# Two delays of a hand-written planner in a one-core decoder layer: the first attention scores come one block later, the first group-norm transposes ask for a later slot

## The chip, the cores and the metric

The kernel runs on one core of a Trainium2 chip. The metric is device time in microseconds, from the start of the execution to its end on that core. Three runs of the kernel before took 410.61, 412.03 and 411.76 us; their median is 411.76 us. One more execution was profiled, and all rows below are from it.

## The reference

One decoder layer is computed for 256 tokens of width 1024. Two kinds of token mixing run side by side on one normalised input: a recurrence with 8 heads (RWKV-7) and softmax attention with 8 heads; a merge with gates, an output projection and a gated MLP follow. The parts that the change touches, shortened:

```python
def step(state, inp):                      # one token of the recurrence
    r_t, w_t, k_t, v_t, a_t, b_t = inp
    sa = jnp.einsum('bhvk,bhk->bhv', state, a_t)
    state = (state * w_t[:, :, None, :] + sa[..., None] * b_t[:, :, None, :]
             + v_t[..., None] * k_t[:, :, None, :])
    return state, jnp.einsum('bhvk,bhk->bhv', state, r_t)
...
mu = jnp.mean(y, axis=-1, keepdims=True)   # group norm over each head's 64 values
var = jnp.mean(jnp.square(y - mu), axis=-1, keepdims=True)
y = ((y - mu) * lax.rsqrt(var + GN_EPS)).reshape(B, S, C)
y = y * ln_g.astype(f32) + ln_b.astype(f32)
...
s_own = jnp.einsum('bhqd,bhkd->bhqk', q_c, k_own, preferred_element_type=f32) * scale
s_own = jnp.where(causal, s_own, -jnp.inf)
p = jax.nn.softmax(s_all, axis=-1).astype(v.dtype)
```

With 256 tokens there is one attention block, so the attention is plain causal attention over 256 keys.

## The kernel before

**The streamed products.** Every large product is made from weights that stream from HBM in pieces of 512 KB (tile raw). ScalarE rounds a piece to a high part (tile whi, L259), VectorE takes the rest as a low part (tile wlo, L269), and TensorE multiplies both. In the stretch that matters here the products go through wst (L293): one call of its inner loop is a **block** of 12 matmuls, eight of L302 and L304 on the high part and four of L307 on the low part, 128x256 each. A piece of weights gives two blocks. The blocks in this stretch are the gate projections (tile acc, input hx), afterwards the attention's branch projection (input ybh). Buffers are few: 4 of raw, 4 of whi, 3 of wlo.

**The side work.** Between the blocks TensorE gets small matmuls, with VectorE and ScalarE working on their results:

- chain (L551), the recurrence in chunks of 64 tokens. It first inverts small triangular matrices (tile X). L765 multiplies X by G into pp, L770 masks pp into P on VectorE, L782 and L790 multiply P and X into px, and L775 adds px to X on VectorE. Then come four steps, c = 0 to 3. In each, L890 and L895 multiply the state Sn, L898 adds the result to Z0 on VectorE, L902 multiplies Z0 by X, L905 (ScalarE) and L906 (VectorE) copy that to VU, L912 and L924 multiply VU, L917 to L920 make the next state Sn on VectorE, and L929 (ScalarE) copies the chunk's output yt. Step 0 has no state yet and begins at L902.
- group_norm (L845), per chunk: sums and means on VectorE (L852, L853, L855), a square on ScalarE (L856), its sum (L858, L859), a power on GpSimd (L860), the scaling on VectorE (L862), then two transposes on TensorE into pc (L869) and the finish (L872 to L875), which gives yah and yal, the input of the last branch projection.
- attention (L967): queries and keys are transposed into qkT (L976, copied by ScalarE, L977), four transposes in four places. Scores then come in three parts, the first over the first 128 tokens and 8 heads, the other two over the second 128 tokens and 4 heads each. A part is its matmuls (L995, tile ps), the masking on VectorE (L998) and, for the later parts, a copy on ScalarE (L1001), the row maximum on VectorE (L1006, L1007), one exponential per head on ScalarE (L1010), and the normalisation on VectorE (L1012, L1013). L1023 then transposes the weights into ppt, L1024 copies them on ScalarE, and L1035 applies them into po.

**What sets the order.** Three Python generators (chain, gn for the group norm, att for the attention) and bulk, the streamed products, run as threads of a planner at the end of body (L1114 and after). Each yield gives an estimated TensorE cost and a delay. The planner's clock moves by the cost, and the thread may go on once the delay is over. The planner takes the first thread in the list whose time has come, in the order chain, gn, att, bulk; a block of bulk costs 0.33 * 4 = 1.32 units:

```python
cost, lat = next(th[1])
now_t += cost
th[2] = now_t + lat
if cost:
    joined[0] = th[0] != "bulk"
```

So a delay decides after how many blocks a piece of side work is issued, and beside which other side work. The flag joined is true while the last cost came from side work. The group norm holds its transposes until it is true, so that they follow other side work without a block between (L865). TensorE runs its instructions in the planner's order; the order of the instructions on VectorE and ScalarE comes from the same program through the framework's scheduler, and each of these engines runs its own queue in order.

Of the kernel before, what the change touches and what calls it, by code (L numbers as in the profile page):

```python
# [37 lines left out]
def body(tc, x, positions, norm1_g, w_in, rwkv_mu, w_decay_up, decay_bias, w_aaa_up,  # L38
# [5 lines left out]
    with ctx:  # L44
# [12 lines left out]
        def b4(name, shape=(128, 4, 256), dt=F32):  # L57
            return sb.tile(list(shape), dt, name=name, tag="b4", bufs=NB4)
# [5 lines left out]
        def t1(name, shape=(128, 256), dt=F32):  # L64
            return sb.tile(list(shape), dt, name=name, tag="c1", bufs=8)
# [7 lines left out]
        def chp(name="ch"):  # L73
            return ps.tile([128, 512], F32, name=name, tag="ch", bufs=3)

        def atp(name="at"):
            return ps.tile([128, 512], F32, name=name, tag="at", bufs=2)
# [469 lines left out]
        def need(nm, d):  # L547
            while nm not in d:
                yield 0, 0.5

        def chain():  # L551
# [36 lines left out]
            for t in range(2):  # L588
                for ct in range(4):
                    i = 8 * t + 2 * ct  # L590
# [254 lines left out]
            def group_norm():  # L845

                for c in range(4):
                    yield from need(c, ny)
                    y = ny[c]
                    cs = slice(64 * c, 64 * c + 64)  # L850
                    st = sb.tile([128, 3, 4], F32, name="st", tag="st", bufs=2)
                    dve.tensor_reduce(st[:, 0], y, axis=AX.X, op=OP.add)  # L852
                    dve.tensor_scalar(st[:, 0], st[:, 0], -1.0 / N, None, op0=OP.mult)  # L853
                    yc, sq2 = t1("yc", (128, 4, 64)), t1("sq2", (128, 4, 64))
                    dve.tensor_tensor(yc, y, st[:, 0][:, :, None].to_broadcast([128, 4, 64]), op=OP.add)  # L855
                    act.activation(sq2, yc, AF.Square)  # L856
                    yield 0, 0.8
                    dve.tensor_reduce(st[:, 1], sq2, axis=AX.X, op=OP.add)  # L858
                    dve.tensor_scalar(st[:, 1], st[:, 1], N * GN_EPS, None, op0=OP.add)  # L859
                    pool.tensor_tensor(st[:, 2], st[:, 1], mhalf, op=OP.pow)  # L860
                    yield 0, 1.6
                    dve.scalar_tensor_tensor(yc, yc, math.sqrt(N), st[:, 2][:, :, None].to_broadcast([128, 4, 64]),  # L862
                                             op0=OP.mult, op1=OP.mult)
                    yield 0, 1.2 if c < 3 else 2.2
                    while not joined[0] and "chain" not in done:  # L865
                        yield 0, 0.1
                    p = chp("pc").rearrange("p (a n) -> p a n", a=8)
                    for j in range(2):
                        pe.transpose(p[:, 2 * j:2 * j + 2].rearrange("p a n -> p (a n)"),  # L869
                                     yc[:, 2 * j:2 * j + 2].rearrange("p q n -> p (q n)"), ident)  # L870
                    yf = t1("yf", (128, 4, 64))
                    dve.tensor_tensor(yf, p[:, 0:4], A1[:, :, cs], op=OP.mult)  # L872
                    dve.tensor_tensor(yf, yf, A2[:, :, cs], op=OP.add)
                    act.copy(yah_[:, :, cs], yf)
                    dve.tensor_tensor(yal[:, :, cs], yf, yah_[:, :, cs].bitcast(F32), op=OP.subtract)  # L875
                    yield 0.5, 2.0

            threads.insert(1, ["gn", group_norm(), 0.0])
            joined[0] = True
            St = None  # L880
# [83 lines left out]
        def flat3(t):  # L964
            return t.rearrange("p h n -> p (h n)")

        def attention():  # L967
            qkT = []
            for i in range(2):
                dT = b4(f"qkT{i}")  # L970
                for j in range(2):
                    p = atp("pqk").rearrange("p (a t c) -> p a t c", a=2, t=2)
                    for a in range(2):
                        for t in range(2):
                            ct = 2 * j + a
                            pe.transpose(p[:, a, t], flat3(qkv[i][:, t])[:, ct * 128:ct * 128 + 128], ident)  # L976
                    act.copy(dT[:, 2 * j:2 * j + 2].rearrange("p a c -> p (a c)"),  # L977
                             p.rearrange("p a t c -> p (a t c)"))
                    yield 0.4, 1.0
                qkT.append(dT)  # L980
            qT, kT = qkT

# [104 lines left out]
        def bulk():  # L1087
            yield from proj4("k", 4)
            yield from proj4("r", 0)
            def attention_input(i):  # L1090
                qkv.append(b4("qkv", (128, 2, 8, 64)))
                ps_ = [acc(), acc()]
                yield from xst(ps_, hh, hl)
                for t in range(2):
                    finish_qk(ps_[t], i, t)

            while not last_exp:
                yield 0, 0.5
            rope_tables()
            yield from attention_input(0)  # L1100
            yield from proj4("v", 8)
            yield from attention_input(1)
            yield from gates(1, 0)
            yield from attention_input(2)
            threads.insert(1, ["att", attention(), now_t + 3.0])
            for j in range(1, 4):
                yield from gates(1, j)
            for j in range(4):
                yield from gates(0, j)
            while "att" not in done:  # L1110
                yield 0, 1.0
            yield from branch(1, *ybs)
# [155 lines left out]
        j, hb = prev.pop(0)  # L1268
# [47 lines left out]
```

## Time and profile before

| | |
|---|---|
| median of three runs | 411.76 us |
| the profiled execution, its own time | 410.49 us |
| its span in the trace | 408.4 us |
| VectorE busy | 324.8 us (80%) |
| ScalarE busy | 233.0 us (57%) |
| GpSimd busy | 38.8 us (10%) |
| granted TensorE clock | 1.00 in every slice |

The time around the span is 410.49 - 408.4 = 2.1 us. Times in the rows are counted from the span's start. The change touches the stretch from 116 us to 187 us. In a timeline row the first number is the start, the second how long it lasted, then engine, line, operation, output and input tile, the shape, and how many instructions were merged. On TensorE a row's length contains the tail of a matmul in the pipeline, so the step from one piece of work to the next is read from the starts. A float32 matmul of the program shows as two records: 32 matmuls of L782 are x64 in the trace.

### The profile page before, as it was taken

The page shows a single profiled execution, that of the slowest core. Times are in us where ns is not written, and L with a number is a line of the kernel's source. Part 1 is how long each engine was busy: PE and PEld are TensorE (multiplying, and loading weights), DVE is VectorE, ACT ScalarE, POOL GpSimd, SP SyncE. Part 2 cuts the span into 40 slices and gives each one's busy share as a digit, 9 for nine tenths or more (in the row PEclk, how much of TensorE's full clock was granted, in tenths as well). Part 3 has the DMA queues.
Part 4 walks back from the last instruction along what each step waited for, and adds up shares of the span by engine and source line. Part 5 has one row for each costly group of instructions (what it writes and reads, how often), then busy time and mean ns, then how long its engine had stood idle before and what let it go on. Part 6 is the DMA issues. An engine that isn't in the chain of part 4 may idle for free.

```text
span 408.4 us, 8156 instructions
## 1 busy us (share of the span) xinstructions
PE 401.3 (98%) x3199; PEld 354.3 (87%) x3199; DVE 324.8 (80%) x564; ACT 233.0 (57%) x387; POOL 38.8 (10%) x65
## 2 busy tenths in 40 slices
PE   7999999999999999999999999999999999999996
PEld 3999989888989989999988888888888888888885
DVE  3888999899679786777973899968769678697694
ACT  6799655474556756444553876645545555465450
POOL 7910070000400010020010100000000000000000
PEclk9999999999999999999999999999999999999999
DMA  8944555563683353465663556666755666656512
GB/s 246 323 150 154 158 158 160 152 173 99 160 232 92 104 152 104 132 206 189 196 201 115 172 190 202 210 208 184 213 180 167 213 185 201 197 171 207 196 55 103
DMA packets 61990, 70.53 MB, mean 173 GB/s; under 512 B 9421, under 2 KB 52243, under 8 KB 61952
## 3 DMA queue, kind: packets, MB, share of 16 engines
q1 hardware_dynamic: 61104, 69.54, 56.5%
q0 software_dynamic: 832, 0.47, 0.6%
q8 instruction: 25, 0.41, 0.4%
q14 instruction: 13, 0.11, 0.1%
q10 hardware_dynamic: 16, 0.00, 0.0%
HBM read 68.56 MB, written 1.44 MB: 171 GB/s over the span
## 4 chain that ended last, share of the span: by engine, by line
PE 90%; DVE 3%; ACT 3%; issue 2%; DMA 1%; SPq 0%; POOL 0%; DVEq 0%; ACTq 0%
PE acc L1202 15%; PE acc L302 8%; PE acc L1207 8%; PE acc L307 7%; PE acc L304 7%; PE at L1202 5%; PE acc L323 5%; PE acc L327 4%; PE acc L324 4%; PE f L1224 4%; PE f L1222 4%; PE f L1226 4%; PE at L1207 2%; DMA x<-in_x_dram 1%; PE pgr L669 1%
## 5 line engine op out<-in xcount | busy, mean ns | idle before, releaser
L259 ACT CAST whi<-raw 128x1024 fp32r<-128x1024 f32 x121 | 126.9, 1052 | 114.0 <-PE acc L304 22.3
L269 DVE TENSOR_TENSOR wlo<-raw,whi 128x1024 fp32r<-128x1024 f32 x121 | 148.5, 1231 | 30.2 <-PE acc L1207 12.2
L1202 PE MATMUL acc<-hx,whi 128*128 128x512 f32 x264 | 68.2, 393 | 0.0
L302 PE MATMUL acc<-hx,whi 128*128 128x256 f32 x232 | 58.5, 288 | 0.0
L304 PE MATMUL acc<-hx,whi 128*128 128x256 f32 x232 | 56.1, 278 | 0.0
L1202 PEld LDWEIGHTS acc<-hx,whi 128*128 128x128 f32 x264 | 47.0, 188 | 8.1
L302 PEld LDWEIGHTS acc<-hx,whi 128*128 128x128 f32 x232 | 43.6, 188 | 1.8 <-issue 0.8
L304 PEld LDWEIGHTS acc<-hx,whi 128*128 128x128 f32 x232 | 43.7, 188 | 0.1
L1207 PEld LDWEIGHTS acc<-h,wlo 128*128 128x128 f32 x264 | 37.1, 188 | 3.6
L1207 PE MATMUL acc<-h,wlo 128*128 128x256 f32 x264 | 37.9, 279 | 0.0
L307 PE MATMUL acc<-hx,wlo 128*128 128x256 f32 x232 | 35.9, 277 | 0.0
L1224 PE MATMUL f<-whi,hb 128*128 128x512 f32 x80 | 31.2, 390 | 0.0
L1226 PE MATMUL f<-wlo,hb 128*128 128x512 f32 x80 | 31.2, 390 | 0.0
L1222 PE MATMUL f<-whi,hb 128*128 128x512 f32 x80 | 31.2, 389 | 0.0
L307 PEld LDWEIGHTS acc<-hx,wlo 128*128 128x128 f32 x232 | 30.7, 188 | 0.3 <-issue 0.3
L1202 PE MATMUL at<-hx,whi 128*128 128x512 f32 x88 | 24.0, 392 | 0.0
L1212 DVE TENSOR_REDUCE an<-acc 128x256 f32<-128x512 f32 x22 | 14.2, 685 | 9.3 <-PE acc L1207 9.3
L1202 PEld LDWEIGHTS at<-hx,whi 128*128 128x128 f32 x88 | 16.4, 188 | 3.6
L323 PE MATMUL acc<-whi,hx 128*128 128x512 f32 x48 | 19.1, 398 | 0.0
L324 PE MATMUL acc<-whi,hx 128*128 128x512 f32 x48 | 18.8, 391 | 0.0
L1226 PEld LDWEIGHTS f<-wlo,hb 128*128 128x128 f32 x80 | 15.0, 188 | 3.1
L1222 PEld LDWEIGHTS f<-whi,hb 128*128 128x128 f32 x80 | 15.0, 188 | 2.8
(322 smaller groups left out, 695.7 us busy)
## 6 DMA issues: line engine op xcount, KB each, us to landing
raw<-in_w_ffn_up_dram SPq DMA_DIRECT2D x44, 512.0 KB, 4.3
raw<-in_w_in_dram SPq DMA_DIRECT2D x37, 512.0 KB, 4.4
raw<-in_w_ffn_down_dram SPq DMA_DIRECT2D x22, 512.0 KB, 4.1
raw<-in_w_out_dram SPq DMA_DIRECT2D x8, 512.0 KB, 4.3
x<-in_x_dram SPq DMA_DIRECT2D x8, 256.0 KB, 4.0
early<-in_w_in_dram SPq DMA_DIRECT2D x4, 512.0 KB, 7.5
raw<-in_w_branch_b_dram SPq DMA_DIRECT2D x4, 512.0 KB, 3.7
raw<-in_w_branch_a_dram SPq DMA_DIRECT2D x4, 512.0 KB, 4.6
```

The source lines that it names most:

```text
L259: act.copy(wide(hi, k, c), spread(raw, k, c))
L269: eng.tensor_tensor(wide(lo, k, c), spread(raw, k, c), wide(hi, k, c).bitcast(F32), op=OP.subtract)
L302: pe.matmul(om, wh[:, k, ms], xh[:, k0 + k], start=k0 + k + m == 0, stop=False, skip_group_check=True)
L304: pe.matmul(om, wh[:, k, ms], xl[:, k0 + k], start=False, stop=False, skip_group_check=True)
L307: pe.matmul(om, wl[:, k, ms], xh[:, k0 + k], start=False, stop=k0 + k == nk - 1 and m == n - 1, skip_group_check=True)
L323: pe.matmul(ps_[t], xh[:, K, ts], wh[:, k], start=K == 0, stop=False)
L324: pe.matmul(ps_[t], xl[:, K, ts], wh[:, k], start=False, stop=False)
L1202: pe.matmul(ps_[m], wh[:, k, m * 128:m * 128 + 128], hx[:, k0 + k].rearrange("p a s -> p (a s)"), start=k0 + k == 0, stop=False, skip_grou ...
L1207: pe.matmul(ps_[m][:, 0:S], wl[:, k, m * 128:m * 128 + 128], h2[k0 // 4][:, k], start=False, stop=k0 + k == 7, skip_group_check=True)
L1222: pe.matmul(fin[f], hb[:, 0, i, ts], wh[:, 0, cs], start=st, stop=False, skip_group_check=f == 3)
L1224: pe.matmul(fin[f], hb[:, 1, i, ts], wh[:, 0, cs], start=False, stop=False, skip_group_check=f == 3)
L1226: pe.matmul(fin[f], hb[:, 0, i, ts], wl[:, 0, cs], start=False, stop=False, skip_group_check=f == 3)
```

## The change

Two delays of the planner change. No instruction is added, removed or resized. The fourth and last of the attention's query and key transposes (i and j both 1) is followed by a delay of 5.5 in place of 1.0, and the group norm of chunk 0 asks for its transposes 4.0 after its scaling in place of 1.2; chunks 1 to 3 keep theirs.

```diff
@@ -861,7 +861,7 @@
                     yield 0, 1.6
                     dve.scalar_tensor_tensor(yc, yc, math.sqrt(N), st[:, 2][:, :, None].to_broadcast([128, 4, 64]),
                                              op0=OP.mult, op1=OP.mult)
-                    yield 0, 1.2 if c < 3 else 2.2
+                    yield 0, (4.0, 1.2, 1.2, 2.2)[c]
                     while not joined[0] and "chain" not in done:
                         yield 0, 0.1
                     p = chp("pc").rearrange("p (a n) -> p a n", a=8)
@@ -976,7 +976,7 @@
                             pe.transpose(p[:, a, t], flat3(qkv[i][:, t])[:, ct * 128:ct * 128 + 128], ident)
                     act.copy(dT[:, 2 * j:2 * j + 2].rearrange("p a c -> p (a c)"),
                              p.rearrange("p a t c -> p (a t c)"))
-                    yield 0.4, 1.0
+                    yield 0.4, 5.5 if i and j else 1.0
                 qkT.append(dT)
             qT, kT = qkT
```

What moves is seen in the engines' queues. With [B] for a block, TensorE's order from the last L976 on was: [B], scores 1 with L782 and L790, [B] [B], L765 with L790 and scores 2, [B] [B], L790, [B], scores 3, [B], L902, [B] [B], L912 and L924, [B] [B], L890 and L895, [B], L1023 with L902 and L869. It becomes: [B] [B], L782 and L790, [B], scores 1, [B], L765 and L790, [B], scores 2, [B], L790, [B] [B], L902 with scores 3, [B] [B], L912 and L924, [B] [B], L890 and L895, [B] [B], L902 with L1023 and L869. From there on the groups are the same in both, with one block more ahead of them.

The first place is TensorE at the first scores, about 117.7 us. Before, they stood at the head of the recurrence's group:

```order
L307 MATMUL acc<-hx,wlo 128x256 x4
L995 MATMUL ps<-qkT_1572,qkT_1505 128x128 x8
L782 MATMUL px<-P,X 64x64 x32
L790 MATMUL px<-X,P 64x64 x16
L302 MATMUL acc<-hx,whi 128x256
```

After the change the same eight matmuls have a block in front and a block behind; L782 and L790 stand one block ahead of these rows:

```order
L304 MATMUL acc<-hx,whi 128x256
L307 MATMUL acc<-hx,wlo 128x256 x4
L995 MATMUL ps<-qkT_1572,qkT_1505 128x128 x8
L302 MATMUL acc<-hx,whi 128x256
L304 MATMUL acc<-hx,whi 128x256
```

The group of L782 and L790 has gone behind a second block and the first scores another block further, into a place of their own.

The second place is VectorE ahead of L898, the addition to Z0 that L902 of step 1 reads. Before, from the mean's subtraction in the group norm of chunk 0 (L855) on:

```order
L855 TENSOR_TENSOR yc<-yt,st 128x256
L1013 TENSOR_TENSOR sc_1645<-sc_1645,sm 128x1024
L858 TENSOR_REDUCE st<-sq_2015 128x4
L269 TENSOR_TENSOR wlo<-raw,whi 128x1024
L859 TENSOR_SCALAR st<-st 128x4
L898 TENSOR_TENSOR Z_1241<-pb,Z_1241 128x128 x2
L862 SCALAR_TENSOR_TENSOR yc<-yc,st 128x256
```

And after the change (sc_1729 is the scores' tile of parts 2 and 3 there):

```order
L855 TENSOR_TENSOR yc<-yt,st 128x256
L858 TENSOR_REDUCE st<-sq_2027 128x4
L859 TENSOR_SCALAR st<-st 128x4
L862 SCALAR_TENSOR_TENSOR yc<-yc,st 128x256
L1012 RECIPROCAL sm<-sm 128x4
L269 TENSOR_TENSOR wlo<-raw,whi 128x1024
L1013 TENSOR_TENSOR sc_1729<-sc_1729,sm 128x1024
L898 TENSOR_TENSOR Z_1241<-pb,Z_1241 128x128 x2
```

L898 has moved from ahead of the group norm's scaling (L862) to behind it, and behind a low part and the normalisation of the last scores as well.

The third place is TensorE at step 1's L902 and the first transposes of the group norm (L869, tile pc). Before:

```order
L307 MATMUL acc<-hx,wlo 128x256 x4
L1023 MATMUL ppt<-ident,sc 128x128 x8
L902 MATMUL pb<-Z_1241,X 64x64 x8
L869 MATMUL pc<-ident,yc 128x128 x2
L302 MATMUL acc<-hx,whi 128x256
```

And after:

```order
L307 MATMUL acc<-hx,wlo 128x256 x4
L902 MATMUL pb<-Z_1241,X 64x64 x8
L1023 MATMUL ppt<-ident,sc 128x128 x8
L869 MATMUL pc<-ident,yc 128x128 x2
L302 MATMUL acc<-hx,whi 128x256
```

L902 now stands ahead of the transposes of the attention weights, and these stand between L902 and L869. The edit in group_norm alone accounts only for the order of L1023 and L869: with the edit in attention alone the group reads L902, L869, L1023.

## The prediction

> **What bounds the kernel now.** I read the page's busy shares and its chain first, then TensorE's timeline from 116 to 187 us, then those of VectorE and ScalarE.
>
> ```profile
> span 408.4 us, 8156 instructions
> PE 401.3 (98%) x3199; PEld 354.3 (87%) x3199; DVE 324.8 (80%) x564; ACT 233.0 (57%) x387; POOL 38.8 (10%) x65
> PE 90%; DVE 3%; ACT 3%; issue 2%; DMA 1%; SPq 0%; POOL 0%; DVEq 0%; ACTq 0%
> ```
>
> TensorE is busy for 98% of the span and is 90% of the chain that ended last. No work is added, so the change is priced by TensorE's steps and by the waits that it gains or loses. Two waits stand in the stretch that moves:
>
> ```profile
> 117.75 1.16 PE L995 MATMUL ps<-qkT,qkT 64*128 64x128 f32 x16
> 118.84 1.16 PE L782 MATMUL px<-P,X 64*64 64x64 f32 x64
> 119.82 0.86 PE L790 MATMUL px<-X,P 64*64 64x64 f32 x23
> 121.33 0.45 PE L790 MATMUL px<-X,P 64*64 64x64 f32 x9 [0.66 <-issue]
> q8 instruction: 1, 0.02, 1.1%
> 147.34 0.46 PE L902 MATMUL pb<-Z,X 64*64 64x64 f32 x16
> 148.29 0.41 PE L869 MATMUL pc<-ident,yc 128*128 128x128 f32 x2 [0.49 <-DVE yc L862]
> ```
>
> The first, 0.66 us inside L790, has no releaser ("issue"). The q8 row is of the DMA queues between 117 and 123 us: one packet of instructions arrived there. I read the gap as TensorE out of instructions. The second, 0.49 us ahead of L869, waits for the group norm's scaling.
>
> **The steps of TensorE.** These starts give the length of each piece; L302 rows are the first matmul of a block.
>
> ```profile
> 124.66 1.16 PE L765 MATMUL pp<-X,G 64*64 64x64 f32 x64
> 127.73 0.39 PE L302 MATMUL acc<-hx,whi 128*128 128x256 f32 x1
> 130.66 2.08 PE L790 MATMUL px<-X,P 64*64 64x64 f32 x64
> 132.68 0.38 PE L302 MATMUL acc<-hx,whi 128*128 128x256 f32 x1
> 134.25 1.14 PE L995 MATMUL ps<-qkT,qkT 64*128 64x256 f32 x8
> 135.31 0.39 PE L302 MATMUL acc<-hx,whi 128*128 128x256 f32 x1
> 140.24 0.69 PE L912 MATMUL pS<-VU,KBt 128*64 128x64 f32 x16
> 144.88 0.38 PE L302 MATMUL acc<-hx,whi 128*128 128x256 f32 x1
> ```
>
> A lone block between two side groups takes 134.25 - 132.68 = 1.57 us, a pair 130.66 - 127.73 = 2.93. Two lone blocks are 3.14, so splitting a pair costs 0.21. Scores alone take 135.31 - 134.25 = 1.06; L765, L790 and scores together 127.73 - 124.66 = 3.07, so L765 and L790 alone 2.01; a pair and the 64 records of L790 132.68 - 127.73 = 4.95; L912, L924, a pair, L890 and L895 144.88 - 140.24 = 4.64.
>
> **The change part by part.** *One more group.* Before, 17 side groups stand between the last L976 and the last L869, after it 18: the first scores had company, now they stand alone. **+0.21 us**, not hidden, since TensorE is the bound.
>
> *The gap for instructions.* Before, TensorE ran dry after 16 + 64 + 23 = 103 records from 117.75 us and went on at 121.33. After, the same 103 records are a block's 12, L782's 64 and 27 of L790. The block ends near 117.75 - 0.09 + 1.45 = 119.1 (a pair's second half, less the half switch ahead of it), L782 takes 119.82 - 118.84 = 0.98, and 27 records at 2.02 / 64 = 0.032 take 0.86: dry at 120.95. If the packet arrives when it did, 0.38 us of gap are left where starts show 121.33 - (119.82 + 23 x 0.032) = 0.78 before: **-0.4 us**, between -0.66 (gap gone) and +0.66 (as long again elsewhere, since blocks of code fall on other work).
> The Trainium skill ("Runtime: NRT & Kernel Launch", section "Instruction fetch mechanics") states that instructions come by DMA in 16 KiB blocks of 256 and that crossing a block is mostly hidden. The packet's size agrees; the hiding does not show at this gap. By the rule this term would be zero and the sum 0.4 us higher.
>
> *The group norm's edit.* L869 is behind L902 in both versions; the edit alone only puts L1023 between them. It hides the 0.49 us wait for L862, if that is done by then, and below it is, by far: **-0.5 us**. If that cover goes, the 0.49 stays.
>
> *What is late next.* VectorE and ScalarE run in order, and the scores are now issued later while the same L902 and L898 follow. Their rows:
>
> ```profile
> 120.02 1.28 DVE L998 TENSOR_TENSOR sc<-ps,cmask 128x512 f32<-128x512 f32 x2
> 121.33 1.22 DVE L1006 TENSOR_REDUCE mx<-sc 128x8 f32<-128x1024 f32 x1
> 124.26 0.17 DVE L1007 TENSOR_SCALAR mx<-mx 128x8 f32<-128x8 f32 x1
> 127.08 0.68 DVE L775 TENSOR_TENSOR X<-X,px 128x512 f32<-128x512 f32 x1
> 127.68 0.20 DVE L1012 RECIPROCAL sm<-sm 128x8 f32<-128x8 f32 x1
> 127.92 1.23 DVE L1013 TENSOR_TENSOR sc<-sc,sm 128x1024 f32<-128x1024 f32 x1
> 129.06 0.75 DVE L998 TENSOR_TENSOR sc<-ps,cmask 128x256 f32<-128x256 f32 x2
> 129.73 1.22 DVE L269 TENSOR_TENSOR wlo<-raw,whi 128x1024 fp32r<-128x1024 f32 x1
> 132.39 0.17 DVE L1007 TENSOR_SCALAR mx<-mx 128x4 f32<-128x4 f32 x1
> 134.77 0.18 DVE L1012 RECIPROCAL sm<-sm 128x4 f32<-128x4 f32 x1 [1.02 <-ACT sc L1010]
> 137.26 0.75 DVE L998 TENSOR_TENSOR sc<-ps,cmask 128x256 f32<-128x256 f32 x2
> 138.45 1.22 DVE L1006 TENSOR_REDUCE mx<-sc 128x4 f32<-128x1024 f32 x1 [0.44 <-ACT sc L1001]
> 139.59 0.47 DVE L906 COPY VU<-pb 64x128 f32<-64x128 f32 x2
> 141.18 0.41 DVE L917 TENSOR_TENSOR Sn<-pS,PC 128x256 f32<-128x256 f32 x1
> 142.38 0.42 DVE L852 TENSOR_REDUCE st<-yt 128x4 f32<-128x256 f32 x1 [0.79 <-ACT yt L929]
> 143.04 0.43 DVE L855 TENSOR_TENSOR yc<-yt,st 128x256 f32<-128x256 f32 x1
> 154.50 0.42 ACT L856 ACTIVATE sq<-yc 128x256 f32<-128x256 f32 x1
> 154.96 0.42 DVE L858 TENSOR_REDUCE st<-sq 128x4 f32<-128x256 f32 x1
> 156.71 0.42 DVE L862 SCALAR_TENSOR_TENSOR yc<-yc,st 128x256 f32<-128x256 f32 x1 [1.13 <-POOL st L860]
> 157.06 0.48 DVE L898 TENSOR_TENSOR Z<-pb,Z 128x128 f32<-128x128 f32 x2
> ```
>
> An operation of 1.22 or 1.23 us steps 1.14 (127.92 to 129.06); L269, L1006 and L1013 are all of that size.
>
> TensorE after the change: L790 ends with its last five records near 121.6, a block to 123.2, the first scores to 124.2. Then block 1.57, L765 and L790 2.01, block 1.57, scores 1.06, block 1.57, L790 and a pair 4.95, L902 0.4, scores 1.06, pair 2.93, L912 to L895 4.64, pair 2.93: 24.7 us. TensorE **asks for L902 of step 1 at 148.9**.
>
> VectorE from the end of the first scores, 124.3, in its new order, which is waited for all the way:
> - L998 1.31, L1006 1.14, L269 1.14: L1007 at 127.9.
> - Eight exponentials on ScalarE, from L1007 to L1012, 127.68 - 124.26 = 3.42: 131.3. (L770 and an L775 fit into this.)
> - L1012 0.24, L1013 1.14, L998 0.67, L269 1.14, L775 0.60, L1006 1.14, L775 0.60: 5.53, so 136.9. Step 0's L902 reads this X; TensorE asks at 136.8, so up to **+0.1 us**.
> - Four exponentials, 134.77 - 132.39 = 2.38. L905 stands behind them on ScalarE and L906 behind L905, some 0.2 more: 139.5.
> - L906 0.4, L1012 0.2, L1013 1.14, L998 to L1006 1.19, L1006 1.14, L269 1.14, L917 and L1007 0.4: L852 at 145.1.
> - L852 to L855 0.66. ScalarE squares behind two exponentials of part 3, half of 2.38 after 145.0, so at 146.2; L858 0.46 later; L862 156.71 - 154.96 = 1.75 after that, the power on GpSimd among it: 148.4.
> - L862 0.35, L1012 0.2, L269 and L1013 2.28, L898 0.48: **L898 done at 151.7**.
>
> TensorE stands from 149.0 to 151.7, and L902's followers, all the blocks too, stand behind it in its queue: **+2.7 us**. The trace of before has no such wait; there L898 was ahead of L862 and L1013. Its ends are 0 and 3.5: nothing if VectorE gains 2.7 us in 27, and 3.5 if each of the three waits on ScalarE and GpSimd is 0.25 longer. I take 2.7, as every step has a row.
>
> After that VectorE is behind again at step 2 (L862 and an L269 ahead of L898), but there a group of po and ppt and two blocks lie between on TensorE; by the same steps L898 is done 0.6 us before L902 asks. The last transposes of the group norm keep their place ahead of the last branch, three blocks in place of four, with 0.5 us to spare. Weights are not late: each wlo is made two blocks or more ahead.
>
> **Sum.** 0.21 - 0.4 - 0.5 + 0.1 + 2.7 = **+2.1 us**, so 410.49 + 2.1 = 412.6 for the profiled execution. The median of the three runs is 1.27 us above that execution; I put the change on the median: 411.76 + 2.1 = **413.9 us**. About 0.3%, 1.24 us, is what a measurement of this kernel can tell from no change.
>
> **The rivals.** *No new wait.* VectorE reaches L898 before TensorE asks, and the three small terms stay with the gap at -0.4: 0.21 - 0.4 - 0.5 = -0.7, 411.1 us, not slower. For it: the longest wait for VectorE on TensorE in this stretch was 0.49 us. Against: it decides at 2.7 us less over 27 us of steps, and only the waits for exponentials and the power are not VectorE's own length. Chance 0.17.
>
> *A second wait at step 2.* The 0.6 us of cover go if ScalarE's copies of ppt push L856 back by more than that; a miss of 1.4 adds 0.8: 414.7 us. For: three copies stand around L856 there; against: GpSimd's power is the longer leg. Chance 0.12.
>
> *A slower clock after the wait.* TensorE's opening matmuls show a slower rate:
>
> ```profile
> 1.45 3.60 PE L109 MATMUL idle<-ones 128*128 128x512 bf16 x8 [1.45 <-DVE eps L374]
> 46.39 0.63 PE L327 MATMUL acc<-wlo,hx 128*128 128x512 f32 x2
> ```
>
> Eight of 512 columns take 3.60 us, 0.45 each, against at most 0.31 later. If the wait brings that rate back for 3.6 us, 8 matmuls' worth, the price is up to 8 x (0.45 - 0.31) = 1.1 to, with the tail left out, 1.8 us: 415.0 to 415.7. The recorded clock speaks against it; the wait of 0.66 left no trace in it. Chance 0.06.
> The Trainium skill ("TensorE: Matmul & The Clock Gate", section "What's actually happening") states that the clock halves after an idle window of about 3.4 us; by that rule 2.7 us are too short, which no row here shows.
>
> *The change moves nothing that counts*, gains and losses cancel: 411.8 us, chance 0.03.
>
> **How the numbers follow.** The forecast has 0.62, with a range of its own of 412.8 to 414.8 (the wait 1.6 to 3.5). The whole range is **410.9 to 415.9**: its low end takes in the rival without a wait, its high end the slower clock. Faster by over 0.3% needs the first rival and more of the gap than -0.4: 0.10 with misses of the reading. Within 0.3%: most of that rival, the last one, and a wait under 1.9 us: 0.26. Slower: 0.64.
>
> **What would show it.** TensorE's row of L902 in step 1 with an idle of 2 to 3.5 us from L898; L898 about 27 us behind the first L998; no idle ahead of the first L869; 0.2 to 0.5 us of "issue" left in L790 near 121 us; no wait at L902 of step 2. The prediction is wrong if L898 of step 1 starts before the second of the two blocks ahead of it ends.

## The result, and the profile after

| | before | after |
|---|---|---|
| median (9 runs each, taken together) | 411.47 us | 414.6 us |
| lowest and highest | 410.61 to 412.59 us | 412.78 to 416.34 us |
| the profiled execution | 410.49 us | 414.42 us |
| its span | 408.4 us | 412.6 us |
| mean granted TensorE clock in it | 1.000 | 0.995 |

The changed kernel is slower: the ratio is 1.0083, with a 95% interval from 1.0064 to 1.0103. The prediction said 413.9 us and slower. The time around the span is 1.8 us here (414.42 - 412.6) where it was 2.1 before, so the two profiled times differ by 3.9 us and their spans by 4.2.

The page of the changed kernel first: the span, the busy shares, the chain that ended last, and the clock in its 40 slices.

```profile
span 412.6 us, 8150 instructions
PE 402.6 (98%) x3199; PEld 355.6 (86%) x3199; DVE 325.8 (79%) x564; ACT 233.1 (56%) x387; POOL 39.1 (9%) x65
PEclk9999999999999989999999999999999999999999
PE 89%; DVE 4%; ACT 3%; issue 2%; DMA 1%; SPq 0%; POOL 0%; DVEq 0%; ACTq 0%; POOLq 0%
```

The shares hardly differ from those of before. Two things do: VectorE has 4% of the chain instead of 3%, and one slice of the clock, the fifteenth (144 to 155 us), shows 8 instead of 9. TensorE's timeline leads to the same place, and these rows hold every idle time that the view gives for TensorE between 116 and 190 us:

```profile
120.52 0.98 PE L790 MATMUL px<-X,P 64*64 64x64 f32 x27
121.80 0.34 PE L790 MATMUL px<-X,P 64*64 64x64 f32 x5 [0.31 <-issue]
137.53 0.46 PE L902 MATMUL pb<-Z,X 64*64 64x64 f32 x16
148.95 0.62 PE L307 MATMUL acc<-hx,wlo 128*128 128x256 f32 x4
152.43 0.90 PE L902 MATMUL pb<-Z,X 64*64 64x64 f32 x16 [2.87 <-DVE Z L898]
153.26 1.97 PE L1023 MATMUL ppt<-ident,sc 128*128 128x128 f32 x8
155.02 0.63 PE L869 MATMUL pc<-ident,yc 128*128 128x128 f32 x2
157.19 0.69 PE L912 MATMUL pS<-VU,KBt 128*64 128x64 f32 x16
164.69 0.46 PE L902 MATMUL pb<-Z,X 64*64 64x64 f32 x16
```

L902 of step 1 waits 2.87 us for L898. The two waits of before are smaller or gone: 0.31 us of "issue" in L790 where there were 0.66, and no idle ahead of L869. The rows behind the wait are long: eight matmuls of L1023 take 1.97 us here, and 1.04 in the row of before:

```profile
146.37 1.04 PE L1023 MATMUL ppt<-ident,sc 128*128 128x128 f32 x8
```

The stretch cut into windows gives the reason. The columns are the window, its length, busy time and records of TensorE's matmuls and weight loads, of VectorE, ScalarE and GpSimd, then the granted clock, the DMA share and GB/s:

```profile
148.00:152.40 4.40, 1.56 (x14) 1.36 (x13) 2.98 (x6) 2.54 (x5) 1.04 (x1) 1.00 0.19 54
152.40:153.50 1.10, 1.07 (x17) 0.94 (x18) 1.10 (x2) 0.13 (x1) 0.00 (x0) 0.59 0.79 264
153.50:154.50 1.00, 1.00 (x6) 1.00 (x6) 0.69 (x3) 0.39 (x3) 0.00 (x0) 0.50 0.59 206
154.50:155.50 1.00, 1.00 (x7) 1.00 (x6) 0.00 (x0) 0.73 (x2) 0.00 (x0) 0.50 0.48 86
155.50:156.50 1.00, 1.00 (x8) 1.00 (x8) 0.78 (x2) 0.35 (x1) 0.00 (x0) 0.75 1.05 369
156.50:157.50 1.00, 1.00 (x17) 0.87 (x17) 0.50 (x2) 0.41 (x1) 0.00 (x0) 1.00 0.20 70
```

During the idle the clock still stands at 1.00. It falls to 0.50 about 0.2 us behind the start of L902 (1.00 in the window from 152.30 to 152.50, 0.50 from 152.70 on), and returns near 156.0 us, 3.4 us later. The lost shares add up to 0.41 x 1.1 + 0.5 + 0.5 + 0.25 = 1.7 us of full speed.

**Where the 4.2 us of span came from.** Two rows of each kernel mark the stretch, the last transposes of the queries and keys and the last ones of the group norm. Those of before stand first, those of after behind the dots:

```profile
115.78 0.66 PE L976 MATMUL pqk<-ident,qkv 128*128 128x128 f32 x4
...
181.68 0.38 PE L869 MATMUL pc<-ident,yc 128*128 128x128 f32 x2
```

```profile
116.21 0.66 PE L976 MATMUL pqk<-ident,qkv 128*128 128x128 f32 x4
...
187.34 0.38 PE L869 MATMUL pc<-ident,yc 128*128 128x128 f32 x2
```

The stretch took 65.90 us and takes 71.13. One block that used to follow it now lies inside: behind it 408.4 - 181.68 = 226.72 us were left, now 412.6 - 187.34 = 225.26. So 5.23 - 1.46 = 3.77 us are the stretch's own. The other 0.43 is ahead of it, where the change touches nothing: in the table of waits, xt (L414, the kernel's first transposes) waits 1.8 us in this execution and 0.9 in that of before. Much of it is scatter: over three profiles of each kernel (e8 to e11 below) the last L976 starts between 115.66 and 115.90 us before, and between 115.88 and 116.21 after. The 3.77 are the wait with 2.87, the slower clock with 1.56 (measured below), the new group with 0.21 as predicted, less 0.36 for the gap (0.78 to 0.42, both from the starts as the prediction counted: 121.80 - (120.52 + 27 x 0.032) = 0.42) and 0.49 for L869's wait: 3.79.

### The profile page after: what moved, and what is told of

The parts are those of the page before. It is cut to its first block, busy times and chain, and to the rows that moved or that the text cites. A ratio compares the mean times of both kernels' runs of the same rounds, so it can differ in the third digit from the quotient of the medians.

```text
span 412.6 us, 8150 instructions
## 1 busy us (share of the span) xinstructions
PE 402.6 (98%) x3199; PEld 355.6 (86%) x3199; DVE 325.8 (79%) x564; ACT 233.1 (56%) x387; POOL 39.1 (9%) x65
## 4 chain that ended last, share of the span: by engine, by line
PE 89%; DVE 4%; ACT 3%; issue 2%; DMA 1%; SPq 0%; POOL 0%; DVEq 0%; ACTq 0%; POOLq 0%
PE acc L1202 15%; PE acc L302 8%; PE acc L1207 7%; PE acc L304 7%; PE acc L307 7%; PE at L1202 5%; PE acc L323 5%; PE acc L327 4%; PE acc L324 4%; PE f L1222 4%; PE f L1224 4%; PE f L1226 4%; PE at L1207 2%; ACT sc L1010 2%; DMA x<-in_x_dram 1%
## 5 line engine op out<-in xcount | busy, mean ns | idle before, releaser
L269 DVE TENSOR_TENSOR wlo<-raw,whi 128x1024 fp32r<-128x1024 f32 x121 | 148.6, 1233 | 28.7 <-PE acc L1207 12.2
```

What stands on the lines that cost most here:

```text
L269: eng.tensor_tensor(wide(lo, k, c), spread(raw, k, c), wide(hi, k, c).bitcast(F32), op=OP.subtract)
```

## Experiments

The theory after the result: the wait stands on the order of VectorE's queue ahead of L898, the slower clock follows from the wait's length, and the group norm's edit costs nothing. The rivals: the group norm's edit has a share; contention from the transfers that come with the wait's end, and not the idle, slows TensorE; the small terms of the sum are scatter.

The first four experiments ran on one chip, beside 21 runs of the kernel before with a median of 411.04 us; the next three, on a second chip, beside 29 with 410.92. Lines of a changed file move: L858, L862, L869, L898 and L902 of the text stand as L859, L863, L870, L899 and L904 in e3, e6 and e7; L902, L912 and L1023 stand as L906, L916 and L1027 in e4; L1013 stands as L1015 in e6.

### e1: the attention's edit alone

```diff
-                    yield 0, (4.0, 1.2, 1.2, 2.2)[c]
+                    yield 0, 1.2 if c < 3 else 2.2
```

> Only the attention's delay of 5.5 is kept; the group norm's delay is 1.2 again, so TensorE's group at step 1 reads L902, L869, L1023. Theory (the loss is the wait of L902 for L898, and the half clock behind it; the group norm's edit is worth nothing): as the changed kernel, 2.9 us of wait at L902 of step 1, half clock behind it, 414 to 415.5 us. Rival (the group norm's edit takes part in the loss or the gain): over 1 us away from the changed kernel.

Measured: 413.72 us, ratio 1.0059 (1.0037 to 1.0082), 0.3 us below the range expected. In the profile the wait is the same to the hundredth, and the clock is as slow (0.58 in 152 to 156 us, against 0.57). L790's gap is 0.87 us here. The clock did not fall in every run: of the four, two have a mean clock of 0.996 (413.88 and 413.60 us) and two of 0.999 (413.85 and 412.84 us), as runs of the kernel before have too.

```profile
121.25 0.33 PE L790 MATMUL px<-X,P 64*64 64x64 f32 x5 [0.87 <-issue]
151.88 0.65 PE L902 MATMUL pb<-Z,X 64*64 64x64 f32 x16 [2.87 <-DVE Z L898]
152.46 0.58 PE L869 MATMUL pc<-ident,yc 128*128 128x128 f32 x2
```

The attention's edit brings the whole wait. L869 has no idle here either: the wait at L902 gave L862 its time, so the group norm's edit was not needed to hide it.

### e2: the normalisation of the last scores behind L898

The reciprocal and the product of part 3 (L1012, L1013) are taken out of softmax and issued after the first weights are applied.

```diff
+                sms.append(sm)
+                if j == 0:
+                    normalised(t, j, nh, sc)
+
+            def normalised(t, j, nh, sc):
+                sm, nk = sms.pop(0), 128 * (t + 1)
                 dve.reciprocal(sm, sm)
...
             weighted(0, p0)
+            normalised(*parts[2])
```

> The changed kernel with the last scores' normalisation (reciprocal and product, 1.2 us on VectorE) issued later, just ahead of the transposes of the second half, so that L898 no longer stands behind it; TensorE's order is unchanged. Theory: L898 is 1.2 us earlier, the wait at L902 of step 1 falls from 2.9 to about 1.7 us; if the clock falls only after a longer idle, it stays at 1.00 and 3 us are gained, 411.8 us; if not, 413.2. Rival (the loss is the order of TensorE's groups): no gain, 414.6.

Measured: 412.97 us, ratio 1.0044 (1.0022 to 1.0065). The rows of TensorE, and its window behind the wait:

```profile
138.02 0.45 PE L902 MATMUL pb<-Z,X 64*64 64x64 f32 x14 [0.78 <-DVE X L775]
151.76 0.65 PE L902 MATMUL pb<-Z,X 64*64 64x64 f32 x16 [1.71 <-DVE Z L898]
...
152.00:156.00 4.00, 4.00 (x38) 3.93 (x36) 3.51 (x6) 1.91 (x5) 0.00 (x0) 0.67 0.47 152
```

The wait fell by 1.16 us, the step of one L1013, so that operation stood in L898's way. The clock falls after 1.71 us of idle too, though not in every run (only the profiled one's wait is known): of the ten runs six have a mean clock of 0.996 (412.63 to 413.81 us), four have 1.0 (410.44, 410.52, 412.68 and 412.75 us). The first row shows a wait that no profile had before: step 0's L902 for X. In this profile the view shows no gap in L790, so TensorE comes there earlier.

### e3: L898 ahead of the sum and the power as well

To e2's edit come two delays exchanged and an explicit order: the group norm's L858 to L860 of chunk 0 are issued behind L898 of step 1.

```diff
-                    yield 0, 0.8
-                    dve.tensor_reduce(st[:, 1], sq2, axis=AX.X, op=OP.add)
+                    yield 0, 0.8 if c else 4.0
+                    with (tc.issue_after(zadd[0]) if c == 0 else ExitStack()):
+                        dve.tensor_reduce(st[:, 1], sq2, axis=AX.X, op=OP.add)
...
-                    yield 0, (4.0, 1.2, 1.2, 2.2)[c]
+                    yield 0, (0.8, 1.2, 1.2, 2.2)[c]
```

> As the kernel with the late normalisation, and the group norm of chunk 0 is held back on VectorE from its second sum on until L898 of step 1 is issued (its delays are exchanged, 4.0 after the square and 0.8 after the scaling). L898 stands behind one low part alone; TensorE's order is that of the changed kernel. Theory: no wait at L902 of step 1 (0 to 0.3), clock 1.00, and the small terms of the prediction are left: 0.4 to 1 us under the kernel before, 410.5 to 411. Rival (order of TensorE's groups): 414 or more.

Measured: 410.12 us, ratio 0.9982 (0.9969 to 0.9996). VectorE's rows first, then TensorE's:

```profile
147.16 0.48 DVE L899 TENSOR_TENSOR Z<-pb,Z 128x128 f32<-128x128 f32 x2
147.56 0.41 DVE L859 TENSOR_REDUCE st<-sq 128x4 f32<-128x256 f32 x1
150.25 0.43 DVE L863 SCALAR_TENSOR_TENSOR yc<-yc,st 128x256 f32<-128x256 f32 x1 [0.93 <-POOL st L861]
...
148.92 0.46 PE L904 MATMUL pb<-Z,X 64*64 64x64 f32 x16
150.73 0.44 PE L870 MATMUL pc<-ident,yc 128*128 128x128 f32 x2 [0.32 <-DVE yc L863]
152.00:156.00 4.00, 3.90 (x65) 3.56 (x65) 3.39 (x10) 1.66 (x5) 0.00 (x0) 1.00 0.40 135
```

L898 (here L899) is done at 147.6, more than a microsecond before TensorE asks at 148.9. Without the wait the clock stays at 1.00, and the time is 0.92 us under that of the runs of before beside it.

### e4: the idle filled with work

Ten matmuls of 512 columns, with no use for the result, stand ahead of L902 of step 1; the wait for L898 stays.

```diff
+                if c == 1:
+                    wb = acc("wb")
+                    for _ in range(10):
+                        pe.matmul(wb, ones[:, 0:128], ones, start=True, stop=True)
```

> The changed kernel with ten matmuls of 512 columns (bf16, on constants, into a spare accumulator, result unused) just ahead of L902 of step 1, some 2.2 us of TensorE's time in the wait; the wait itself is not removed. Theory (the slow matmuls behind the wait are a clock lowered by the idle time): L902 starts when it did, some 0.6 us of idle are left, clock 1.00, L902 to the next block at full speed, 1.7 us gained: 413 us. Rival (they are slow from contention with transfers or other engines): they stay slow, 414.6 or more.

Measured: 412.77 us, ratio 1.0042 (1.0026 to 1.0058).

```profile
149.89 2.10 PE L903 MATMUL wb<-ones 128*128 128x512 bf16 x9
152.70 0.65 PE L906 MATMUL pb<-Z,X 64*64 64x64 f32 x16 [0.70 <-DVE Z L898]
153.28 1.09 PE L1027 MATMUL ppt<-ident,sc 128*128 128x128 f32 x8
155.90 0.69 PE L916 MATMUL pS<-VU,KBt 128*64 128x64 f32 x16
152.00:156.00 4.00, 3.30 (x40) 3.10 (x42) 3.23 (x9) 1.91 (x5) 0.00 (x0) 1.00 0.57 188
```

L902 starts as late as in the changed kernel, 152.70 against 152.43, and the same work follows, but at full speed: L902 to L912 takes 155.90 - 152.70 = 3.20 us, in the changed kernel 157.19 - 152.43 = 4.76. The slow clock costs 1.56 us there. The DMA share in these 4 us is near to that of the changed kernel (0.57 against 0.66), so contention with transfers is not the cause; with TensorE's idle time filled, the slow clock is gone. The median gained 0.95 us on e1, less than the 1.56 of the two profiles, for two of e1's four runs had no fall of the clock to lose; the gap in L790 (0.87 in e1's profile, none shown in this) and the kernel's start scatter by as much.

### e5: the group norm's edit alone

```diff
-                    yield 0.4, 5.5 if i and j else 1.0
+                    yield 0.4, 1.0
```

> The group norm's delay alone (4.0 in place of 1.2 for chunk 0), on the kernel before. Theory A (of the two edits the attention's alone brings the wait at step 1's L902, and the group norm's edit only changes where the first transposes stand): no wait for VectorE of over 0.6 us at any L902, granted clock 1.00 from 116 to 190 us, and the 0.66 us of issue inside L790 at about 121 us stays as in the kernel before, since the order there is that of before; time within 0.6 us of before. Rival B (the group norm's edit has a share in the slowdown): a wait of 1 us or more in the stretch from 145 to 165 us and 1.5 us or more on the time.

Measured: 410.88 us, ratio 0.9996 (0.9978 to 1.0014), no wait for VectorE of over 0.2 us at TensorE between 116 and 190 us, and a clock of 1.00 there. The first theory holds on all but one point: the view shows no gap in L790, although the order ahead of it is that of before.

```profile
120.44 1.25 PE L790 MATMUL px<-X,P 64*64 64x64 f32 x32
148.40 0.46 PE L902 MATMUL pb<-Z,X 64*64 64x64 f32 x16
153.24 0.44 PE L869 MATMUL pc<-ident,yc 128*128 128x128 f32 x2
```

Without the attention's edit, L869 falls behind a later group (the one with L924). The 0.49 us wait is gone, and the time shows no gain from it within the interval of 0.7 us either way.

### e6: only the sum and the power behind L898

The changed kernel with e3's edit of the group norm, without e2's. The expectation places the normalisation between the two halves of L898 in the changed kernel too; VectorE's rows have it ahead of both there, and only in e6 between them.

> The changed kernel with chunk 0's sum of squares and power held behind the addition to Z0 (L898) and the two delays of chunk 0 exchanged; the normalisation of the last scores stays where the change put it, between the two halves of L898. Theory A (the 2.87 us at step 1's L902 are VectorE's own work ahead of L898 plus its wait of 1.57 us for GpSimd's power; the clock falls after an idle of TensorE between 0.7 and 1.7 us): the wait at L902 falls to 0.2 to 0.8 us, the granted clock stays at 1.00 in 152 to 156 us, time within 0.8 us of before. Rival B (only the normalisation of the last scores keeps L898 late, as its move took 1.16 us off): the wait stays at 1.7 us or more, the clock falls to about 0.6 to 0.7 in that stretch, time 2 us or more over before.

Measured: 411.95 us, ratio 1.0015 (0.9996 to 1.0033).

```profile
122.76 0.34 PE L790 MATMUL px<-X,P 64*64 64x64 f32 x5 [1.26 <-issue]
150.45 0.91 PE L904 MATMUL pb<-Z,X 64*64 64x64 f32 x16
153.43 0.44 PE L870 MATMUL pc<-ident,yc 128*128 128x128 f32 x2 [1.05 <-DVE yc L863]
...
149.25 0.26 DVE L899 TENSOR_TENSOR Z<-pb,Z 128x128 f32<-128x128 f32 x1
149.43 1.21 DVE L1015 TENSOR_TENSOR sc<-sc,sm 128x1024 f32<-128x1024 f32 x1
150.56 0.28 DVE L899 TENSOR_TENSOR Z<-pb,Z 128x128 f32<-128x128 f32 x1
...
152.00:156.00 4.00, 2.83 (x39) 2.43 (x39) 2.71 (x6) 1.33 (x3) 0.91 (x1) 1.00 0.07 25
```

The view shows no idle ahead of L902, but its row is 0.91 long where 0.46 is usual: some 0.45 us of wait lie inside it, as the second half of L898 comes late, behind the normalisation. The clock stays at 1.00, and so it does after 1.26 us without instructions (1.00 in the windows 120 to 124 and 124 to 130 us). The normalisation alone is thus not what holds L898; the larger share is the group norm's sum and scaling with VectorE's stand of 1.57 us for GpSimd between them, all of which are behind L898 here. The time misses the first theory's bound of 0.8 us over before by 0.2: L869's wait grew to 1.05 us, as its scaling now comes last.

### e7: e3's kernel again

> The kernel in which L898 of step 1 goes ahead of the group norm's sum of squares and of the last scores' normalisation, a second time, on whatever chip this is. Theory A (without the wait and the slower clock the change is worth the sum of its small terms, 0.2 - 0.4 - 0.5 = -0.7 us): 0.4 to 1.2 us under before. Rival B (the first look was scatter between 409.6 and 412.2 us): within 0.3 us of before or above it.

Measured: 410.15 us, ratio 0.9982 (0.9964 to 0.9999), 0.77 us under before. Both times the interval ends just below 1. Some 0.3 of the 0.8 us lie outside the span: time less span is 2.04 to 2.18 us in the runs of before beside e3 and e7, and 1.74 to 1.86 in those of every changed kernel, with or without the wait. What the rest is made of is not shown: in e7's profile L902 of step 0 waits 0.93 us for X, and e3's stretch of 67.17 us (from its marks at 115.83 and 183.00) is only 0.2 shorter than that of before with the extra block, 65.90 + 1.46 = 67.36.

### e8 to e11: two more profiles of each kernel, unchanged

> The kernel before, unchanged, profiled a second time, to see how much of the gap inside L790 belongs to the order of the instructions. Theory A (the gap of 0.66 us follows from how many records stand ahead of it, as the prediction counted): 23 records, a gap of 0.5 to 0.8 us at about 121 us, then 9 records. Rival B (whether a gap shows is decided by when the packet of instructions arrives, which differs from one execution to the next): the break stays behind 23 records where there is one, but the gap lies anywhere from 0 to 1.3 us.

> The changed kernel, unchanged, profiled a second time. Theory A (the order sets the gap): 27 records, 0.2 to 0.5 us, 5 records in L790. Rival B (the execution sets it): anything from 0 to 1.3 us, with a wait of up to 0.9 us for X at step 0's L902 where there is no gap. In both: 2.6 to 3.1 us ahead of step 1's L902, and a granted clock of 0.5 to 0.7 in the 4 us behind it.

> The kernel before, unchanged, profiled a third time: as in the second profile. If its gap differs from the second's by more than 0.3 us, the term of the sum for the gap cannot be read from one profile of each kernel.

> The changed kernel, unchanged, profiled a third time: as in its second profile. If the time from the last of the query and key transposes to the last transposes of the group norm, less the waits and the slow clock, agrees within 0.3 us over its three profiles, the scatter of the times lies in the start of the kernel and in this gap.

Measured, one profile each, with the first profile of each kernel for comparison (all in us; "packet" is the start of the packet of instructions, queue q8 in the DMA records of the trace, and "goes on" the start of L790's second row, both counted from the start of the last L976; "rest" is the stretch without the gap and without the wait at L869 or L902):

| profile | records ahead of the gap | packet | goes on | gap | wait at L902 | L902 to L912 | stretch | rest | time |
|---|---|---|---|---|---|---|---|---|---|
| before | 23 | 3.05 | 5.55 | 0.66 | none | | 65.90 | 64.75 | 410.49 |
| e8 | 23 | 3.89 | 6.32 | 1.42 | none | | 66.75 | 64.84 | 411.26 |
| e10 | 23 | 3.17 | 5.62 | 0.72 | none | | 66.05 | 64.84 | 410.71 |
| after | 27 | 3.10 | 5.59 | 0.31 | 2.87 | 4.76 | 71.13 | 67.95 | 414.42 |
| e9 | 27 | 3.06 | 5.60 | 0.32 | 2.89 | 4.82 | 71.28 | 68.07 | 414.38 |
| e11 | 27 | 3.43 | 5.87 | 0.59 | 2.88 | 4.61 | 71.51 | 68.04 | 414.43 |

The break is always behind the same record, and the rest agrees within 0.12 us for each kernel. The gap's size differs by up to 0.76 us between executions of one kernel; e8's 1.42 lies above what either theory allowed, and as e8 and e10 differ by 0.70, the term of the sum for the gap cannot be read from one profile of each kernel. Its mean is 0.93 before and 0.41 after. Both theories have a share: the order sets where TensorE runs dry, the execution when the packet comes.

The packets show the second share. TensorE goes on 2.4 to 2.5 us after the packet's start in all six, and 2.4 and 2.6 us after it in e1 and e6. In e2, e5 and e7, which show no gap, the packet starts 2.9 to 3.7 us before TensorE has run the records ahead of the break (27, in e5 23, at 0.032 each). In e3 and e4 it starts 2.3 and 2.4 us before, and L790's row of 32 records is 1.43 and 1.18 us long where 1.10 is usual, so a small gap lies inside. The gap is thus what is left of some 2.5 us when TensorE comes to that record. Over the 13 profiles the packet starts 1.5 to 4.0 us behind the last L976; why it comes when it does is open.

The clock in 152 to 156 us was 0.64 and 0.75 in e9 and e11; the second is above the 0.5 to 0.7 expected.

## Why the prediction was right, point by point

**One more group, +0.21.** Not measured alone. It fits: the rests differ by 68.02 - 64.81 = 3.21 us in the mean; less a block (1.46) and the slow clock (4.73 - 3.20 = 1.53 in the mean), some 0.2 are left.

**The gap for instructions, -0.4.** Right in the mechanism: dry after 27 of L790's 32 records, and by the same count from the starts 0.42 us left against the 0.38 reckoned. That the size came out is luck, for the working let the packet arrive when it did before, and its start differs by more than the term between executions. Over three profiles of each kernel the means differ by 0.52, but e1's gap with the new order was 0.87, e6's 1.26, e2 and e7 had none, and e5 had none with the order of before. A gain of 0.4 is not shown.

**The group norm's edit, -0.5.** The wait did go, but e1 shows it gone without that edit, and e5 shows no gain in time from it alone. The reason given, that L1023 covers it, was not what mattered: L902's wait covers it.

**X late at step 0, up to +0.1.** Not there in the three profiles of the changed kernel. It is tied to the gap: in e2 and e7, which had no gap, TensorE stood 0.78 and 0.93 us for X. A gap saved there can be a wait here, though e4 had neither and e3 a small gap inside its row and no wait.

**The wait at L902, +2.7.** Right in place, cause and size. VectorE's rows of the changed kernel:

```profile
124.84 1.29 DVE L998 TENSOR_TENSOR sc<-ps,cmask 128x512 f32<-128x512 f32 x2 [0.67 <-PE ps L995]
147.68 0.17 DVE L859 TENSOR_SCALAR st<-st 128x4 f32<-128x4 f32 x1
149.42 0.43 DVE L862 SCALAR_TENSOR_TENSOR yc<-yc,st 128x256 f32<-128x256 f32 x1 [1.57 <-POOL st L860]
149.85 1.19 DVE L269 TENSOR_TENSOR wlo<-raw,whi 128x1024 fp32r<-128x1024 f32 x1
150.96 1.22 DVE L1013 TENSOR_TENSOR sc<-sc,sm 128x1024 f32<-128x1024 f32 x1
152.09 0.48 DVE L898 TENSOR_TENSOR Z<-pb,Z 128x128 f32<-128x128 f32 x2
```

From the first L998 to L898 it took 152.09 - 124.84 = 27.25 us, against about 27 predicted. The steps on the way fit as well, so the sum is not right by errors that cancel: L1012 of part 1 at 131.85 us against 131.3, L906 at 140.00 against 139.5, L852 at 145.60 against 145.1, all some 0.5 late, as this execution came to the stretch 0.43 later. L862 at 149.42 against 148.4 lost another 0.5. The last 4.4 us hold three things ahead of L898: the stand for GpSimd's power, an L269 and L1013. Taking L1013 away gave 1.16 us (e2), taking the stand away, with the normalisation between L898's halves, left some 0.45 of wait (e6), both together left none (e3).

**After that.** No wait at step 2: L898 starts at 163.72 there, 1.0 us ahead of L902, done half a microsecond before it, where 0.6 was predicted. The last L869 has no idle.

**What the sum lacked: the slower clock.** The prediction had it as a rival of 0.06 and priced it at 1.1 to 1.8 us. The price was right (1.56), and the chance was not: eight of the nine runs of the changed kernel have a mean clock of 0.992 to 0.996, and the ninth, with 1.0, is the fastest at 412.78 us. Two of the eight, at 0.992, lost about 0.008 x 413 = 3.3 us of clock, twice what the profiled one lost; no trace shows where. The step that failed is the remark that the recorded clock speaks against it since the idle of 0.66 us had left no trace. An idle of 0.66 says nothing of one four times as long. Nor does the recorded clock show every slow stretch: it stands at 1.00 from 2 to 4 us, where the opening matmuls take 0.45 us each, and e4's of the same form (128x512, bf16) take 2.10 / 9 = 0.23. The prediction had set the 0.45 beside float32 matmuls of 0.31. With this term the forecast would have been 2.1 + 1.6 = 3.7 us above before; the medians differ by 3.1, the profiled times by 3.9, the profiled spans by 4.2, of which 0.43 belong to the start. So what happened is the forecast's wait and the rival's slow clock together, and that the stated time was only 0.7 us too low is luck in part: the change of the medians was 1.0 more than forecast, and the median of before came out 0.3 lower over nine runs than over three.

The Trainium skill ("TensorE: Matmul & The Clock Gate", section "What's actually happening") gives an idle window of about 3.4 us for the clock to halve, and as long a busy one for it to return. The return agrees: the lost 1.7 us of clock at half speed are 3.4 us. The fall does not: idles of 2.87 to 2.89 us were enough in all four profiles that have them and, by the mean clock, in eight runs of nine of the changed kernel and two of four of e1; 1.71 us were enough in e2's profile, and by the mean clock in six of its ten runs; 1.26 and 1.42 us (e6, e8) left the clock at 1.00. The measurement decides.

## What to carry to other kernels

Before an instruction is moved on the engine that sets the time, walk the helper engines' queues, which run in order: the addition that TensorE needed had been put behind a scaling that waits for a third engine and behind two operations of 1.2 us, and one stand of 2.9 us outweighed all gains. An idle of TensorE can cost more than its length: those of 1.7 and 2.9 us here brought some 1.5 us of slow clock on top in most executions, so count it as likely and not as a remote rival. Gaps for instructions vary between executions of one kernel by more than a small edit gains, so take several profiles of each, and look up when the packet came, before crediting an edit with one.

## What the runs showed of the hardware that was not expected

The granted clock fell to 0.50 after idles of 2.87 and even 1.71 us and stayed down for about 3.4 us in all five profiles that show it, and the work behind the idle took 4.76 us in place of 3.20. The fall shows only behind the idle, never during it, and not at once: in windows of 0.25 us it came 0.2 us behind the start of L902 in the changed kernel's first profile, 0.7 in e1, 0.9 in e9, 1.5 in e11 and 1.6 in e2.

TensorE ran out of instructions at the same record in each execution that showed a gap for a given order, for 0.31 to 1.42 us, and went on 2.4 to 2.6 us after the packet of instructions had started; where the packet started 2.9 us or more before that record was reached, there was no gap.
